# Issuing the last store of a batched matmul-subtract from ScalarE's queue, behind the main section

## The chip, the cores and the metric

The kernel runs on one core of a Trainium2 chip. The metric is the device time of one execution in microseconds (us). Runs of the kernel are given by their median; one further execution was recorded by the hardware profiler, and all times inside the kernel come from that recording.

## The reference

```python
def setup_inputs():
    batch, m, k, n = 16, 512, 1024, 768
    return {
        "x": np.random.randn(batch, m, k).astype(np.float32),
        "weight": np.random.randn(k, n).astype(np.float32),
        "sub_value": np.random.randn(batch, m, n).astype(np.float32),
    }

def reference(x, weight, sub_value):
    return (np.matmul(x, weight) - sub_value).astype(np.float32)
```

One weight matrix is shared by the whole batch, so this is a product of 8192 x 1024 by 1024 x 768 with an elementwise subtraction behind it.

## The kernel before

The 8192 rows are cut into 64 tiles of 128 rows. For each tile, `x` comes in as float32; ScalarE casts it to float16 (line 324); TensorE transposes it (line 342) and ScalarE copies the result back (line 355), or, for some pairs of tiles, VectorE transposes it in blocks (line 375). TensorE then multiplies it with the resident float16 weights into a PSUM accumulator (lines 199 and 404). VectorE subtracts (line 424): it reads the accumulator and the tile's `sub_value` from `so_ring` and writes the result over `sub_value` in the same ring. The result is stored from there.

All transfers are listed in `TRANSFERS`, in the order in which they are issued: kind (`x`, `w` for the weights, `s` for `sub_value`, `o` for the output), first tile, number of tiles. `issue()` goes down this list and puts each transfer on SyncE's queue (line 304; line 264 for the weights). A store waits for the count of subtractions, `finish`. The last three stores are five tiles (56 to 60, 1920 KB), two tiles (61 and 62, 768 KB) and one tile (63, 384 KB). In a store, each row of a tile goes to its own place in the output, 128 partitions at a time.

Besides these, ScalarE issues one small transfer at the very start (line 177): 16 rows of 128 bytes from `sub_value` into the output, which later stores overwrite. The stores wait for it (`touched`).

Each transfer raises a semaphore by 16 when it has landed: each of the 16 DMA engines raises it by one. `lane` hands out these semaphores and takes one again when the transfers that used it are known to have landed; `known` collects those. At the end of the kernel, the lanes that hold transfers not yet known to have landed are `left`; one of them, `last`, is that of the last store.

The instructions are first collected per engine and then written out in one critical section (`section`), whose waits are all placed by hand. When a section closes, SyncE signals the other engines; each of them passes a drain (GpSimd a no-op) and signals back; SyncE waits for all of these and passes on. Behind the sections the framework adds a closing part: SyncE drains, all engines meet in a barrier, GpSimd clears the semaphores, and all meet once more.

Before the change, SyncE waits inside the main section for all of `left` but `last` (line 531), then closes the section (line 532), and waits for `last` alone in a second section that only SyncE has work in (lines 533 and 534). In the profile, the waits of the second section and the closing part carry line 560, and some of the signals of the sections the lines 137 and 533.

Of the kernel before, what the change touches and what calls it, by code (L numbers as in the profile page):

```python
# [104 lines left out]
def kernel(  # L105
# [7 lines left out]
    nc = tc.nc  # L113
# [7 lines left out]
    n_mt = M_TOT // P  # L121
# [5 lines left out]
    def view(flat, at, n):  # L127

        first, size = next(one for one in SEGMENTS if one[0] <= at < sum(one))
        assert at + n <= first + size  # L130
        rows = flat[first * P : (first + size) * P].rearrange("(p j) c -> p j c", p=P, j=size)
        return rows[:, at - first : at - first + n]
# [36 lines left out]
    def count(name):  # L169
        so_far[name] += 1  # L170
        return (counter[name], 1)
# [11 lines left out]
        out=along, data0=ones, data1=ones, initial=0.0, op0=mybir.AluOpType.mult, op1=mybir.AluOpType.add,  # L183
    ), waits=[(counter["ident"], 1)], then=count("ident"))
    dve.add(lambda: nc.vector.transpose(across, along), waits=[(counter["ident"], 3)], then=count("ident"))  # L185
    for a in range(P // Q):
        here = slice(a * Q, (a + 1) * Q)
        dve.add(lambda here=here: nc.vector.tensor_tensor(  # L188
            out=ident[here, here], in0=along[here], in1=across[here], op=mybir.AluOpType.is_equal,
# [33 lines left out]
    todo = list(TRANSFERS)  # L223
# [3 lines left out]
    lanes = []  # L227
    of_x, of_s, of_o = {}, {}, {}
    known = set()

    def lane(tag):

        for one in lanes:
            if one["tags"] <= known:
                break
        else:
            one = {"sem": tc.alloc_semaphore(f"lane{len(lanes)}"), "value": 0, "tags": set()}
            lanes.append(one)
        one["value"] += 16
        one["tags"].add(tag)  # L240
        return one["sem"], one["value"]

    def issue():
        nonlocal known, from_w
        while todo:
            kind, at, n = todo[0]
            span = set(range(at, at + n))
            old = {t - NX if kind == "x" else t - NSO for t in span}
            need, by = {
                "w": (set(), "o"),  # L250
                "x": ({t for t in old if t >= 0}, "cast"),
                "s": ({t for t in old if t >= 0}, "o"),
                "o": (span, "finish"),
            }[kind]
            if not need <= done[by]:
                return
            todo.pop(0)
            done[kind] |= span
            if kind == "w":

                first = NSO - 2 * (n_c - at)
                st = so_ring[:, first : first + 2 * n]
                sem, value = lane((kind, at))
                sp.add(lambda st=st, at=at, n=n: nc.sync.dma_start(out=st, in_=w_rows[:, 2 * at : 2 * (at + n)]), then=(sem, 16))  # L264
                for c in range(at, at + n):
                    for r in range(2):
                        here = so_ring[:, first + 2 * (c - at) + r]
                        dve.add(
                            lambda c=c, r=r, here=here: nc.vector.tensor_copy(out=w_sb[:, c, r], in_=here),  # L269
                            waits=[(sem, value)], then=count("w"),  # L270
                        )
                        staged[first + 2 * (c - at) + r] = so_far["w"]
                    w_at[c] = so_far["w"]
                from_w |= {(("w", at), so_far["w"])}
                continue
            ring, size, flat = {
                "x": (x_ring, NX, x_flat), "s": (so_ring, NSO, sub_flat), "o": (so_ring, NSO, out_flat)
            }[kind]
            here = ring[:, at % size : at % size + n]
            there = view(flat, at, n)  # L280
            waits = []
            if kind == "x" and need:
                waits.append((counter["cast"], max(cast_at[t] for t in need)))
                last = max(need, key=lambda t: cast_at[t])
                known |= {tag for t, tag in of_x.items() if t in cast_at and cast_at[t] <= cast_at[last]}
            if kind == "s":
                for t in need:
                    waits.append(landed["o", t])
                    known.add(of_o[t])
                for t in span:  # L290
                    if t % NSO in staged:
                        waits.append((counter["w"], staged.pop(t % NSO)))
                        known |= {tag for tag, value in from_w if value <= waits[-1][1]}
            if kind == "o":
                waits.append((touched, 16))
                waits.append((counter["finish"], max(finish_at[t] for t in need)))
                known |= {of_s[t] for t in finish_at if finish_at[t] <= max(finish_at[u] for u in need)}
            sem, value = lane((kind, at))
            for t in span:
                landed[kind, t] = (sem, value)  # L300
                {"x": of_x, "s": of_s, "o": of_o}[kind][t] = (kind, at)
            if kind == "o":
                here, there = there, here
            sp.add(lambda here=here, there=there: nc.sync.dma_start(out=here, in_=there), waits, (sem, 16))  # L304

    def cast(mi):
        assert mi in done["x"]
        done["cast"].add(mi)
        x_in = x_ring[:, mi % NX].rearrange("p (q c r) -> p c q r", c=n_c, r=2)
        first = mi - mi % 2  # L310
        waits = [landed["x", mi]]
        if first in ON_DVE:
            if mi == first:
                b, before = take("x16p", N16P, mi)
                if before is not None:
                    waits.append((counter["pair"], pair_at[before]))
            to = x16p_b[:, slot["x16p", first], mi - first]
        else:
            b, before = take("x16", N16, mi)
            if before is not None:  # L320
                waits.append((counter["turn"], turn_at[before]))
            to = x16_b[:, b]
        to = to.rearrange("p (c q r) -> p c q r", c=n_c, r=2)
        act.add(lambda: nc.scalar.copy(out=to, in_=x_in), waits, count("cast"))  # L324
        cast_at[mi] = so_far["cast"]
        issue()
# [92 lines left out]
    def finish(mi):  # L419
        assert mi in done["s"]  # L420
        done["finish"].add(mi)
        o = so_ring[:, mi % NSO].rearrange("p (h n) -> p h n", h=2)
        po = po_b[:, slot["po", mi]]
        dve.add(lambda: nc.vector.tensor_tensor(  # L424
            out=o, in0=po[:, :, :NS], in1=o, op=mybir.AluOpType.subtract
        ), [landed["s", mi], (counter["mul"], mul_at[mi])], count("finish"))
        finish_at[mi] = so_far["finish"]
        issue()

    issue()  # L430


# [91 lines left out]
    pe.emit_loop([pe.ops[a:b] for a, b in zip(ends, ends[1:])])  # L524
    pe.emit(pe.ops[ends[-1] :])

    left = [one for one in lanes if not one["tags"] <= known]
    last = next(one for one in left if of_o[n_mt - 1] in one["tags"])
    for one in left:
        if one is not last:  # L530
            nc.sync.wait_ge(one["sem"], one["value"])
    section.close()
    with tc.tile_critical(sync_engine=mybir.EngineType.SP, no_gpsimd_drain=True):
        nc.sync.wait_ge(last["sem"], last["value"])


# [28 lines left out]
```

## Time and profile before

| what | value |
| --- | --- |
| median of 5 runs | 210.3 us (209.95 to 210.35) |
| profiled execution | 210.22 us |
| its span, first to last instruction | 208.4 us |
| TensorE matmul busy | 196.3 us (94%) |
| VectorE busy | 128.0 us (61%) |
| ScalarE busy | 113.6 us (55%) |
| bytes moved, mean rate | 87.08 MB, 418 GB/s |

The span is what the recording shows of the program's own instructions; the execution's time holds 1.82 us more, which lie around it. Times inside the profile count from the start of the span. Lines such as `L304` are lines of the kernel; `SPq` is SyncE's sequencer (it issues transfers and waits), `ACTq` ScalarE's. A DMA row gives the time from issue to landing, that is, until the semaphore has its full count.

### The profile page before, as it was taken

How to read it: one execution, taken by the hardware profiler on the slowest of the kernel's cores; microseconds unless marked ns; L12 is line 12 of the kernel's file. 1: busy time of each engine (PE TensorE's matmuls, PEld its weight loads, DVE VectorE, ACT ScalarE, POOL GpSimd, SP SyncE). 2: the span in 40 equal slices, each digit the busy share in tenths (PEclk: the TensorE clock that was granted, in tenths of full speed). 3: DMA queues.
4: the chain of work that ended last, by engine and by line, in shares of the span. 5: the costliest groups of instructions: out<-in, count | busy, mean ns of one | idle time of the engine just before them, and what ended most of it. 6: DMA issues, size and time to landing. Idle time of an engine off the chain costs nothing.

```text
span 208.4 us, 2609 instructions
## 1 busy us (share of the span) xinstructions
PE 196.3 (94%) x1233; PEld 75.6 (36%) x701; DVE 128.0 (61%) x224; ACT 113.6 (55%) x113; POOL 1.0 (0%) x7
## 2 busy tenths in 40 slices
PE   6989699989999999999999999999999999999970
PEld 0133334324434433443443443343344344334320
DVE  2321513975994795598299479559829937953330
ACT  4274688616772862845655586293665738607300
POOL 1000000000000000000000000000000000000000
PEclk9999999999999999999999999999999999999996
DMA  6999999999999899999999999999999999999993
GB/s 214 392 448 417 440 428 424 429 421 451 453 410 478 370 453 434 450 421 407 467 434 418 425 420 439 437 453 415 417 459 418 437 429 415 443 434 425 432 409 145
DMA packets 4932, 87.08 MB, mean 418 GB/s; under 512 B 576, under 2 KB 576, under 8 KB 960
## 3 DMA queue, kind: packets, MB, share of 16 engines
q1 hardware_dynamic: 4896, 87.03, 97.8%
q8 instruction: 1, 0.02, 0.0%
q14 instruction: 3, 0.02, 0.0%
q10 hardware_dynamic: 32, 0.00, 0.0%
HBM read 61.87 MB, written 25.17 MB: 418 GB/s over the span
## 4 chain that ended last, share of the span: by engine, by line
PE 75%; DMA 14%; DVE 6%; SPq 2%; issue 1%; DVEq 0%
PE po_b L199 67%; DMA so_ring<-in_sub_value_dram 14%; PE pt_b L342 8%; DVE xtp_b L375 3%; DVE so_ring L424 2%; SPq L304 1%; SPq L264 0%; SPq L560 0%; DVEq L58 0%; SPq L137 0%
## 5 line engine op out<-in xcount | busy, mean ns | idle before, releaser
L199 PE MATMUL po_b<-w_sb,xt_b 128*128 128x384 f16 x704 | 125.8, 326 | 1.8 <-DVE so_ring L424 1.4
L424 DVE TENSOR_TENSOR so_ring<-po_b,so_ring 128x768 f32<-128x768 f32 x64 | 60.8, 957 | 60.9 <-PE po_b L199 41.9
L355 ACT COPY xt_b<-pt_b 128x1024 f16<-128x1024 f16 x44 | 44.4, 1012 | 62.6 <-PE pt_b L342 62.6
L375 DVE STREAM_TRANSPOSE xtp_b<-x16p_b 32x256 f32<-32x256 f32 x144 | 62.7, 435 | 2.5 <-ACT x16p_b L324 0.3
L199 PE MATMUL po_b<-w_sb,xtp_b 128*128 128x384 f16 x320 | 61.3, 326 | 1.1 <-DVE xtp_b L375 1.0
L404 PEld LDWEIGHTS <-xt_b 128*128 128x128 f16 x352 | 34.4, 98 | 59.0 <-issue 54.0
L324 ACT CAST x_b<-x_ring 128x1024 f16<-128x1024 f32 x46 | 50.6, 1126 | 7.6 <-DMA x_ring<-in_x_dram 7.6
L342 PE MATMUL pt_b<-ident,x_b 128*128 128x128 f32 x184 | 47.4, 274 | 1.1 <-ACT x_b L324 1.1
L342 PEld LDWEIGHTS pt_b<-ident,x_b 128*128 128x128 f32 x184 | 25.3, 141 | 44.9 <-issue 39.4
L324 ACT CAST x16p_b<-x_ring 128x1024 f16<-128x1024 f32 x18 | 20.3, 1126 | 11.0 <-DMA x_ring<-in_x_dram 11.0
L404 PEld LDWEIGHTS <-xtp_b 128*128 128x128 f16 x160 | 15.7, 98 | 19.7 <-issue 17.6
L199 PE MATMUL po_b<-idle_x,idle_w 128*128 128x512 f16 x25 | 8.8, 504 | 1.7 <-POOL idle_x L179 1.7
L269 DVE CAST w_sb<-so_ring 128x768 f16<-128x768 f32 x8 | 3.9, 554 | 10.2 <-DMA so_ring<-in_weight_dram 10.2
L355 ACT COPY xtp_b<-pt_b 128x1024 f16<-128x1024 f16 x2 | 2.0, 1014 | 1.4 <-PE pt_b L342 1.4
L324 ACT ACT_TABLE_LOAD x1 | 1.3, 1283 | 1.6 <-SPq L137 1.6
L434 PEld LDWEIGHTS <-idle_w 128*128 128x128 f16 x5 | 0.5, 99 | 2.1 <-POOL idle_x L179 1.7
L188 DVE TENSOR_TENSOR ident<-along,across 32x32 f32<-32x32 f32 x4 | 0.7, 183 | 0.1
L180 DVE MEMSET ones<- 128x32 f32 x1 | 0.1, 85 | 1.0 <-SPq L137 1.0
L179 POOL MEMSET idle_x<- 128x512 f16 x1 | 0.5, 529 | 0.0
L506 ACT CAST stub<-ident 128x1 f16<-128x1 f32 x2 | 0.4, 192 | 0.0
L185 DVE STREAM_TRANSPOSE across<-along 128x32 f32<-128x32 f32 x1 | 0.2, 211 | 0.0
L483 POOL MEMSET mark<- 128x1 f32 x1 | 0.1, 98 | 25.1 <-ACT xtp_b L355 25.1
(7 smaller groups left out, 1.0 us busy)
## 6 DMA issues: line engine op xcount, KB each, us to landing
so_ring<-in_sub_value_dram SPq DMA_DIRECT2D x7, 3072.0 KB, 24.2
out_dram<-so_ring SPq DMA_DIRECT2D x7, 3072.0 KB, 26.0
x_ring<-in_x_dram SPq DMA_DIRECT2D x5, 4096.0 KB, 22.6
x_ring<-in_x_dram SPq DMA_DIRECT2D x2, 2048.0 KB, 29.4
so_ring<-in_weight_dram SPq DMA_DIRECT2D x2, 1536.0 KB, 9.8
x_ring<-in_x_dram SPq DMA_DIRECT2D x3, 1024.0 KB, 20.6
so_ring<-in_sub_value_dram SPq DMA_DIRECT2D x2, 1536.0 KB, 24.1
x_ring<-in_x_dram SPq DMA_DIRECT2D x1, 3072.0 KB, 27.4
```

Source lines behind the costliest of these rows:

```text
L179: pool.add(lambda: nc.gpsimd.memset(idle_x, 0.0), then=count("idle"))
L188: dve.add(lambda here=here: nc.vector.tensor_tensor(out=ident[here, here], in0=along[here], in1=across[here], op=mybir.AluOpType.is_equal, ...
L199: return nc.tensor.add_instruction(mybir.InstMatmult(name=nc.get_next_instruction_name(), engine=full.engine, ins=list(full.ins), outs=lis ...
L269: lambda c=c, r=r, here=here: nc.vector.tensor_copy(out=w_sb[:, c, r], in_=here),
L304: sp.add(lambda here=here, there=there: nc.sync.dma_start(out=here, in_=there), waits, (sem, 16))
L324: act.add(lambda: nc.scalar.copy(out=to, in_=x_in), waits, count("cast"))
L342: pe.add(lambda: nc.tensor.transpose(words, from_, ident), waits, count("turn") if last else None)
L355: act.add(lambda: nc.scalar.copy(out=to, in_=pt_b[:, b]), waits, count("evac"))
L375: dve.add(lambda: nc.vector.transpose(xt[b * Q : (b + 1) * Q, :, a * Q : (a + 1) * Q], x16[a * Q : (a + 1) * Q, :, b * Q : (b + 1) * Q],), ...
L404: pe.add(lambda weights=weights: nc.tensor.ldweights(weights, tile_position=(0, 0)), [w for w in waits if w[0] in ready])
L424: dve.add(lambda: nc.vector.tensor_tensor(out=o, in0=po[:, :, :NS], in1=o, op=mybir.AluOpType.subtract), [landed["s", mi], (counter["mul"] ...
L434: pe.add(lambda: nc.tensor.ldweights(idle_w, tile_position=(0, 0)), [(counter["idle"], 2)])
```

## The change

The last entry of `TRANSFERS` is no longer put on SyncE's queue. `issue()` keeps its source and destination in `outside` and takes no lane for it. The main section closes without waiting for any store. A second section, named `waited`, follows, in which SyncE waits for every lane that is not known to have landed. After it the kernel issues the last store from ScalarE with a plain `dma_start` that the framework tracks: the framework gives it a semaphore of its own, and SyncE's drain in the closing part waits for that semaphore. `add_manual_dep` puts the store behind `waited` in the order of the program without a wait on it (`NoSync`).

```diff
@@ -227,6 +227,7 @@
     lanes = []
     of_x, of_s, of_o = {}, {}, {}
     known = set()
+    outside = []
 
     def lane(tag):
 
@@ -295,6 +296,9 @@
                 waits.append((touched, 16))
                 waits.append((counter["finish"], max(finish_at[t] for t in need)))
                 known |= {of_s[t] for t in finish_at if finish_at[t] <= max(finish_at[u] for u in need)}
+            if kind == "o" and not todo:
+                outside[:] = there, here
+                return
             sem, value = lane((kind, at))
             for t in span:
                 landed[kind, t] = (sem, value)
@@ -524,14 +528,17 @@
     pe.emit_loop([pe.ops[a:b] for a, b in zip(ends, ends[1:])])
     pe.emit(pe.ops[ends[-1] :])
 
-    left = [one for one in lanes if not one["tags"] <= known]
-    last = next(one for one in left if of_o[n_mt - 1] in one["tags"])
-    for one in left:
-        if one is not last:
-            nc.sync.wait_ge(one["sem"], one["value"])
     section.close()
-    with tc.tile_critical(sync_engine=mybir.EngineType.SP, no_gpsimd_drain=True):
-        nc.sync.wait_ge(last["sem"], last["value"])
+    with tc.tile_critical(sync_engine=mybir.EngineType.SP, no_gpsimd_drain=True) as waited:
+        for one in lanes:
+            if not one["tags"] <= known:
+                nc.sync.wait_ge(one["sem"], one["value"])
+    here, there = outside
+    stored = nc.scalar.dma_start(out=here, in_=there)
+    tc.add_manual_dep(
+        stored.ins, waited.name, mybir.DependencyInfo(mybir.DependencyClass.NoSync, mybir.DependencyReason.DATA),
+        reason="behind the waits",
+    )
 
 
 # ---- launch: one core; inputs and outputs as the reference has them ----
```

In the built program ScalarE's store waits for the count with which SyncE ends the main section, and for nothing else. Behind the second section's waits, SyncE has one branch, one signal, one drain, one no-op and the drain that waits for the last store.

## The prediction

> **What bounds the kernel now.** I read the page first, then the timeline of the last 15 us, the DMA issues, the busy time in short stretches, and SyncE's own waits.
>
> ```profile
> span 208.4 us, 2609 instructions
> PE 196.3 (94%) x1233; PEld 75.6 (36%) x701; DVE 128.0 (61%) x224; ACT 113.6 (55%) x113; POOL 1.0 (0%) x7
> GB/s 214 392 448 417 440 428 424 429 421 451 453 410 478 370 453 434 450 421 407 467 434 418 425 420 439 437 453 415 417 459 418 437 429 415 443 434 425 432 409 145
> q10 hardware_dynamic: 32, 0.00, 0.0%
> PE 75%; DMA 14%; DVE 6%; SPq 2%; issue 1%; DVEq 0%
> ```
>
> TensorE is 94% busy and the DMA engines move some 430 GB/s until the last slices. The change touches nothing before the last subtraction, so only the end matters: what lies behind it.
>
> The timeline (start, duration, engine and line):
>
> ```profile
> 201.91 0.96 DVE L424 TENSOR_TENSOR so_ring<-po_b,so_ring 128x768 f32<-128x768 f32 x1 [1.64 <-PE po_b L199]
> 202.90 0.33 SPq L304 DMA_DIRECT2D out_dram<-so_ring  x1
> ```
>
> The last subtraction ends at 202.87; SyncE starts the last store at 202.90. From there to the end, 208.40, no compute engine is busy. The DMA issues (KB each, us from issue to landing):
>
> ```profile
> out_dram<-so_ring SPq DMA_DIRECT2D x1, 1920.0 KB, 9.8
> out_dram<-so_ring SPq DMA_DIRECT2D x1, 768.0 KB, 5.9
> out_dram<-so_ring SPq DMA_DIRECT2D x1, 384.0 KB, 4.2
> out_dram<-in_sub_value_dram ACTq DMA_DIRECT2D x1, 2.0 KB, 3.6
> ```
>
> The five-tile store (issued 194.55) lands at 204.3, the two-tile store (200.30) at 206.17, the one-tile store (202.90) at 207.12. Busy time by stretch, the last two columns being the DMA share and GB/s:
>
> ```profile
> 204.00:205.00 1.00, 0.00 (x0) 0.00 (x0) 0.00 (x0) 0.00 (x0) 0.00 (x0) 0.95 0.80 323
> 205.00:206.00 1.00, 0.00 (x0) 0.00 (x0) 0.00 (x0) 0.00 (x0) 0.00 (x0) 0.50 0.19 77
> 206.00:207.00 1.00, 0.00 (x0) 0.00 (x0) 0.00 (x0) 0.00 (x0) 0.00 (x0) 0.50 0.08 34
> ```
>
> A share of 0.19 is three of the 16 DMA engines, 0.08 little more than one. In the packet records, 13 engines' shares of the last store land between 205.03 and 205.51, the other three at 206.57, 206.94 and 207.12; the two earlier stores split the same way (three engines 1.1 to 1.7 us behind the rest). So the end hangs on one late DMA engine working off its queue: its share of the five-tile store until 203.98, eight 6,144-byte packets of the two-tile store until 205.82 (0.234 us each), eight 3,072-byte packets of the last until 206.78 (0.121 each), and 0.34 to the landing. SyncE's waits:
>
> ```profile
> SPq L531 <- DMA out_dram<-so_ring: 2.8, 1, 2.8
> SPq L304 <- DVE so_ring L424: 2.3, 1, 2.3
> SPq L560 <- DMA out_dram<-so_ring: 0.2, 1, 0.2
> ```
>
> SyncE sleeps 2.8 us for the two-tile store (L531), closes the main section (206.25 to 206.92), then sleeps 0.16 for the last store. After the landing at 207.12 it still passes a branch (207.18), a signal (207.33), a drain (207.42), a no-op (207.49), a drain (207.54) and the barrier drain (207.60). From there the barrier and the clearing of semaphores take 0.80, to 208.40: landing to end 1.28.
>
> **The change, part by part.** In the built program everything up to the two-tile store is the same, instruction for instruction.
>
> 1. *The last store leaves SyncE's queue and is issued by ScalarE after a handshake.* SyncE closes the section as soon as the two-tile store is issued (200.63) and waits for the drains of the other engines; VectorE's is last, behind the subtraction (202.87). No row shows a VectorE drain behind work; GpSimd's at the start ended 0.05 after its last memset, so 202.92. A semaphore reaches another engine in about 0.03 (the subtraction's end to the store's start: 0.028), so SyncE goes on at 202.95. Two event waits and a no-op, 0.065 apart in the same place of this trace (206.578, 206.642, 206.708), put its signal at 203.09, and ScalarE starts at 203.12: 0.22 later than now. ScalarE has been idle since its last copy (197.8). Nothing is queued behind its wait but the store and the final barrier.
>
> 2. *The issue itself on ScalarE's queue.* The one ScalarE issue of this trace:
>
> ```profile
> L177 ACTq DMA_DIRECT2D out_dram<-in_sub_value_dram x1: 619/619/619, 0.9 to 0.9; - x1
> ```
>
> It took 0.62, where SyncE's first took 0.38 and its late ones 0.33. Bounds: no longer than SyncE's (0.33), or 0.29 more. First packets now come 0.85 after the issue started (203.745), so they come at 203.96 to 204.25. I take 204.1, since the 0.62 was that engine's first. On the 13 quick engines the last store then lands 0.2 to 0.5 later, by 206.0 at most. This costs nothing on the path: the late engine reaches the last store only at 205.83, at least 1.6 after the packets are there. If that cover is gone (all engines level), the 0.22 to 0.51 is paid.
>
> 3. *Two queues instead of one on each DMA engine.* Same bytes, same engines, so the late engine still runs dry near 206.78 and the last of the two stores still lands at 207.12; only the order between them can change. ScalarE's 32 packets at the start (ring 10 on the page) are the row for this. They were issued at 0.90, the first started at 3.593, and on each engine they began as the eight packets of the first load of x ended (3.587 to 4.00), never between them. I therefore take it that a started store is finished first. At 204.1 the late engine has left the five-tile store (203.98) and is inside the two-tile store, so the order stays: two-tile lands 206.17, last 207.12. The margin is 0.12, and -0.02 to 0.27 at the bounds.
>
> The Trainium skill ("DMA: Bandwidth & Descriptors", Queues, rings and completion order) states that each DMA engine goes round its queues and drains a whole packet of some 9 to 17 descriptors before it switches. That speaks against the change: whatever ScalarE queues while an engine is still in the five-tile store would, by the rule, be served before the two-tile store. With arrival at 204.1 the rule gives the same sum as the row, with arrival before 203.98 the sum of the first rival below.
>
> 4. *SyncE's second section waits for the other stores.* Wake-up at 206.185 (two-tile store), five more event waits 0.064 apart (+0.32), branch +0.064, signal +0.155, drain +0.085, no-op +0.073, final drain +0.044: 206.93. It lies under the last store's flight, with 0.19 to spare.
>
> 5. *The end waits only in the final drain.* Landing 207.12, +0.015 to wake, +0.063 to the barrier drain, +0.80: 208.00. Before: 208.40.
>
> The sum: -0.40 (1.28 from landing to end becomes 0.88), with 0.22 to 0.51 of later issue hidden. Span 208.00; the profiled execution took 210.22 for a span of 208.40, so 1.82 lies around it: **209.82**. The median of the runs is 210.30, 0.08 above the profiled one; the same saving from the median would be 209.90.
>
> **The rivals.**
>
> *The last store overtakes the two-tile store on the late engine.* Place: ring order on that one engine. It decides if the packets arrive before the engine leaves the five-tile store (203.98 here, against 203.96 to 204.25), or if engines mix two stores packet by packet. Price: the last store's eight packets go first (0.97), so the two-tile store lands at up to 207.12, and behind it now stands the whole of step 4 (0.76) and the barrier (0.86): end 208.74, +0.34, **210.56**. Mixed packet by packet from 204.1, seven small packets come between: landing near 207.02, end 208.64, 210.46. For it: the margin is smaller than the 0.4 by which runs differ. Against: the start of the kernel shows no mixing, and every cost that I left out of step 1 makes the arrival later.
>
> *ScalarE's queue is slow.* Its one transfer needed 2.69 from issue to first packet; I read that as waiting for x. If it is the queue's own, packets start at 205.81 and the last lands at 207.13 to 207.54 (spread of 0.41 as at the start): 208.0 to 208.4, **209.82 to 210.24**.
>
> *The late engine is not late* in the timed runs. Then 205.51 is the landing before, the 0.22 to 0.51 is paid, and the sum is -0.18 to +0.11: **210.04 to 210.33**. Against: the same three engines' lag shows in all three stores.
>
> *The store really waits for the second section.* ScalarE would issue at about 206.8, landing 2.2 later (0.85, eight packets, 0.34) and 0.88 to the end: 209.9, **211.7**. Against: in the built program ScalarE's store waits for the count that SyncE raises at the end of the first section.
>
> **How the numbers follow.** Chances: forecast 0.60, overtaking 0.20, slow queue 0.11, level engines 0.07, waiting store 0.02. A measurement of this kernel tells 0.2% (0.42 us) from no change, so the bounds are 209.88 and 210.72. The forecast lies right at the first: 209.82 to 209.90, so I give it 0.39 faster and 0.21 same. Overtaking, at 210.56 on the profiled execution and 210.64 on the median, is half same, half slower (0.10 each). Slow queue: 0.03 faster, 0.06 same, 0.02 slower. Level engines same. Waiting store slower. Faster 0.42, same 0.44, slower 0.14. Range: the forecast less 0.3 for the runs' own spread (209.95 to 210.35 before), up to the overtaking case: 209.5 to 210.6; the forecast's own is 209.6 to 210.0.
>
> **What would show it.** ScalarE's store at 203.1 with a duration of 0.33 to 0.62; the two-tile store landing near 206.2 and before the last one; the last still at 207.1; then under 0.9 to the end, and SyncE's last DMA wait in the closing part rather than at L531. If the two-tile store lands within 0.7 of the last or after it, step 3 is wrong; if the last lands after 207.3, step 2 is; if more than 0.95 lies between landing and end, step 5 is.

## The result, and the profile after

| what | before | after |
| --- | --- | --- |
| median | 210.2 us (209.88 to 210.8, 49 runs) | 209.79 us (209.4 to 210.24, 29 runs) |
| ratio, after to before | | 0.9981, 95% interval 0.9976 to 0.9987 |
| profiled execution | 210.22 us, span 208.4 us | 210.04 us, span 208.2 us |

The kernel is 0.19% faster, 0.40 us of 210.2 (0.27 to 0.50 by the interval). The two profiled executions differ by only 0.18 us. That is no contradiction: in the recording of after, the late DMA engine ran 0.22 us later than in that of before, as shown below, and one recording is one draw.

The timeline of after (start, duration, engine and line), where lines 308 and 428 are the old lines 304 and 424:

```profile
200.75 0.33 SPq L308 DMA_DIRECT2D out_dram<-so_ring  x1
202.36 0.96 DVE L428 TENSOR_TENSOR so_ring<-po_b,so_ring 128x768 f32<-128x768 f32 x1 [1.64 <-PE po_b L199]
203.57 0.36 ACTq L537 DMA_DIRECT2D out_dram<-so_ring  x1
```

The last subtraction ends at 203.32 (202.87 in the recording of before), and ScalarE starts the last store 0.25 behind it, where SyncE started it 0.03 behind. The DMA issues of the three last stores (KB, us from issue to landing):

```profile
out_dram<-so_ring SPq DMA_DIRECT2D x1, 1920.0 KB, 9.5
out_dram<-so_ring SPq DMA_DIRECT2D x1, 768.0 KB, 5.6
out_dram<-so_ring ACTq DMA_DIRECT2D x1, 384.0 KB, 3.8
```

200.75 + 5.6 puts the two-tile store's landing at 206.39, 203.57 + 3.8 the last one's at 207.34: the order has stayed, 0.95 apart as before, and both are 0.22 later than before (206.17 and 207.12). Busy time by stretch, the last two columns being the DMA share and GB/s:

```profile
205.00:206.00 1.00, 0.00 (x0) 0.00 (x0) 0.00 (x0) 0.00 (x0) 0.00 (x0) 0.95 0.50 203
206.00:207.00 1.00, 0.00 (x0) 0.00 (x0) 0.00 (x0) 0.00 (x0) 0.00 (x0) 0.50 0.12 49
```

The 13 quick DMA engines now work on the last store until 205.5 (share 0.50 instead of 0.19 in the first row), because its packets came later. Behind 206 only late engines are left, as before (a share of 0.12 is two of the 16 on average; before it was 0.08). The quick engines lost time that nobody waits for. SyncE's waits:

```profile
SPq L535 <- DMA out_dram<-so_ring: 2.8, 1, 2.8
SPq L137 <- DVEq L137: 2.1, 1, 2.1
SPq L567 <- DMA out_dram<-so_ring: 0.2, 1, 0.2
```

L137 is the close of the main section: SyncE waits there for VectorE's drain, before the store and not behind it. L535 is the two-tile store in the second section, and the last row the final drain, which now waits for the last store itself. Its row, with the barrier drain behind it:

```profile
L567 SPq DRAIN  x3: 7/7/7, 207.4 to 207.7; - x3
```

The first of the three is that drain, at 207.354 in the record, and the end is at 208.213. From landing to end: 208.213 - 207.337 = 0.88, where before had 208.396 - 207.118 = 1.28. The difference, 0.40, is the saving that the timed runs show.

### The profile page after: what moved, and what is told of

It is laid out like the page before. It is cut to its first block, busy times and chain, and to the rows that moved or that the text cites. A ratio compares the mean times of both kernels' runs of the same rounds, so it can differ in the third digit from the quotient of the medians.

```text
span 208.2 us, 2608 instructions
## 1 busy us (share of the span) xinstructions
PE 196.3 (94%) x1233; PEld 76.1 (37%) x701; DVE 128.0 (61%) x224; ACT 113.5 (55%) x113; POOL 1.0 (0%) x7
## 4 chain that ended last, share of the span: by engine, by line
PE 89%; DMA 5%; ACT 2%; DVE 0%; SPq 0%; issue 0%
PE po_b L199 80%; PE pt_b L346 9%; DMA x_ring<-in_x_dram 5%; ACT x_b L328 2%; ACT xt_b L359 0%; DVE so_ring L428 0%; ACT xtp_b L359 0%; SPq L265 0%; SPq L308 0%; SPq L567 0%; SPq L137 0%
## 5 line engine op out<-in xcount | busy, mean ns | idle before, releaser
L199 PE MATMUL po_b<-w_sb,xt_b 128*128 128x384 f16 x704 | 127.3, 329 | 3.2 <-DVE w_sb L270 1.8
L199 PE MATMUL po_b<-idle_x,idle_w 128*128 128x512 f16 x25 | 7.6, 445 | 1.7 <-POOL idle_x L179 1.7
```

Source lines behind the costliest of these rows:

```text
L199: return nc.tensor.add_instruction(mybir.InstMatmult(name=nc.get_next_instruction_name(), engine=full.engine, ins=list(full.ins), outs=lis ...
```

## The experiments

Ratios are to the kernel before, timed on the same chip in the same rounds. The spread of a single ratio is about 0.001 either way, 0.2 us.

**ScalarE's queue alone.** In `issue()` of the kernel before, the last store goes to ScalarE, inside the main section:

```diff
+            if kind == "o" and not todo:
+                act.add(lambda here=here, there=there: nc.scalar.dma_start(out=here, in_=there), waits, (sem, 16))
+                return
             sp.add(lambda here=here, there=there: nc.sync.dma_start(out=here, in_=there), waits, (sem, 16))
```

> The kernel before, with one thing changed: the last store is issued by ScalarE inside the main section, as soon as the last subtraction is counted; waits and closing as before. Theory (the change saves 0.40 us because five steps of SyncE between the last landing and the end are gone; ScalarE's queue itself saves nothing): landing to end stays 1.28 us. If the two queues are served in order of arrival, ratio 1.000 to the kernel before (+0.0 us). If an engine takes turns between the queues, the last store's packets come at about 203.75, before the latest DMA engine leaves the five-tile store (203.98), the last store overtakes the two-tile store there, the two-tile store lands near 207.1, and 2.1 us of closing follow it: end near 209.2, +0.8 us, ratio 1.004. Rival (ScalarE's queue, a second queue beside SyncE's, is what saves): -0.4 us, ratio 0.998.

Ratio 1.0000 (0.9991 to 1.0009). The issue and its landing:

```profile
202.62 0.36 ACTq L305 DMA_DIRECT2D out_dram<-so_ring  x1
out_dram<-so_ring ACTq DMA_DIRECT2D x1, 384.0 KB, 4.9
```

Landing 207.51, end 208.79: 1.28 again. ScalarE's queue saves nothing. The DMA view of this kernel, between the issue and 203.8:

```profile
q1 hardware_dynamic: 76, 0.45, 89.2%
q10 hardware_dynamic: 14, 0.04, 8.8%
```

ScalarE's packets (ring 10) are on the quick engines by then, from 203.59. The latest engine leaves the five-tile store only at 204.38 in this recording. So the packets did come first, and still the two-tile store landed at 206.58 and the last at 207.51. Nothing overtook anything: of the expectation's two branches the one with order of arrival holds here.

**The moved waits alone.** All stores stay on SyncE; the second section waits for all of them:

```diff
-    left = [one for one in lanes if not one["tags"] <= known]
...
     section.close()
     with tc.tile_critical(sync_engine=mybir.EngineType.SP, no_gpsimd_drain=True):
-        nc.sync.wait_ge(last["sem"], last["value"])
+        for one in lanes:
+            if not one["tags"] <= known:
+                nc.sync.wait_ge(one["sem"], one["value"])
```

> The kernel before, with the waits for all stores, the last one's too, moved into the second section; all stores stay on SyncE's queue inside the main section. Theory: the handshake of the main section now runs early, but behind the last landing (207.12) stand the wake, five more event waits (0.32), branch, signal, drain, no-op, drain (0.42) and the closing (0.86): landing to end 1.62, +0.34 us, ratio 1.0016. Rival (the early handshake of the main section is what saves): -0.4 us, ratio 0.998.

Ratio 1.0016 (1.0007 to 1.0025), +0.34 us. This half of the change is a loss by itself. SyncE's rows for the second section and the closing:

```profile
L531 SPq EVENT_SEMAPHORE  x2: 17/22/28, 206.7 to 207.7; - x2
...
L557 SPq EVENT_SEMAPHORE  x7: 17/28/28, 207.7 to 209.2; - x7
L557 SPq DRAIN  x3: 7/7/7, 208.4 to 208.7; - x3
```

The wait for the last store ends at 207.67. Five of the event waits of L557 come behind it, 0.06 apart, where nothing hides them (the other two belong to the closing). Landing (207.653) to end (209.265) is 1.61.

**A tracked store on SyncE.** The changed kernel, with the store issued between the sections:

```diff
     section.close()
-    with tc.tile_critical(sync_engine=mybir.EngineType.SP, no_gpsimd_drain=True) as waited:
+    here, there = outside
+    nc.sync.dma_start(out=here, in_=there)
+    with tc.tile_critical(sync_engine=mybir.EngineType.SP, no_gpsimd_drain=True):
...
```

> The changed kernel with the last store issued as a tracked transfer by SyncE, between the main section and the second one. The framework then puts a wait for it at the end of the second section's waits. Theory: issue about 0.2 us later than in the kernel before, hidden by the late DMA engine (landing 207.1); behind the landing stand branch, signal, drain, no-op and two drains again, 1.28 us to the end: +0.0 us, ratio 1.000. Rival (a tracked transfer is what saves, wherever it is waited for): -0.4 us, ratio 0.998. Rival (the later issue costs): +0.2 us, ratio 1.001.

Ratio 0.9995 (0.9986 to 1.0004): no difference to the kernel before. The store was issued 0.28 behind the subtraction and landed at 207.32, the two-tile store 0.95 ahead of it; landing to end 1.32. So tracking is not what saves. It saves only if nothing but the last drain waits for it. Here the framework also put a wait for it into the second section, at its end (at 207.337 in the record), with branch, signal, drain and no-op behind it. SyncE's two waits there, for the two-tile store and for the last one:

```profile
SPq L537 <- DMA out_dram<-so_ring: 2.8, 1, 2.8
SPq L563 <- DMA out_dram<-so_ring: 0.6, 1, 0.6
```

On SyncE the store could stand behind that section only by being issued after its waits, that is, after 206.4. This is what ScalarE's queue is for in the change.

**One more microsecond in front of the store.** The changed kernel, with copies on ScalarE behind the last subtraction, into buffers that nobody reads any more (`n` is 1, then 3):

```diff
     assert not todo
     marks[n_mt] = len(pe.ops)
+    for b in range(n):
+        act.add(lambda b=b: nc.scalar.copy(out=x16_b[:, b], in_=x_ring[:, 0]), [(counter["finish"], so_far["finish"])])
```

> The changed kernel with one more copy of 128x1024 (1.0 to 1.1 us) on ScalarE between the last subtraction and the end of the main section, so that the last store is issued about 1.1 us later. Theory (a late DMA engine reaches the last store only about 1.7 us after its packets are there, so a delay up to that costs nothing): same as the changed kernel, -0.4 us to the kernel before, ratio 0.998, last landing as early as without the copy. Rival (the delay is on the path): +0.7 us to the kernel before, ratio 1.003.

Ratio 0.9979 (0.9970 to 0.9988): as fast as the changed kernel. SyncE waits 0.99 longer for ScalarE's drain, the store is issued 1.21 behind the subtraction, and still lands at 207.10, end 207.98. The delay is hidden.

> The changed kernel with three more copies of 128x1024 (3.0 to 3.4 us in all) on ScalarE between the last subtraction and the end of the main section. Theory: the cover of about 1.7 us is used up; packets come at about 207.1 to 207.4, landing 1.3 us later near 208.5, end near 209.4, +1.0 us to the kernel before (ratio 1.005): of the delay of 3.1 about 1.4 is paid. Rival (the delay is paid whole): +2.7 us, ratio 1.013.

Ratio 1.0018 (1.0006 to 1.0029), +0.38 us. A part of the delay is paid, but less than expected (+1.0). Its profile shows that the cover is used up:

```profile
203.42 2.94 ACT L521 CAST x_b<-x_ring 128x1024 f16<-128x1024 f32 x3 [5.13 <-DVE so_ring L428]
206.49 0.36 ACTq L539 DMA_DIRECT2D out_dram<-so_ring  x1
```

and, by stretch:

```profile
206.00:207.00 1.00, 0.00 (x0) 0.00 (x0) 0.00 (x0) 0.36 (x1) 0.00 (x0) 0.55 0.00 0
207.00:208.00 1.00, 0.00 (x0) 0.00 (x0) 0.00 (x0) 0.00 (x0) 0.00 (x0) 0.50 0.66 267
```

All 16 engines stand still for a microsecond (share 0.00) and then do the last store together, landing 2.3 after its issue. The timed runs pay 0.38 + 0.40 = 0.78 of 2.89 against the changed kernel, so they have a cover of 2.1 (1.8 to 2.4 by the two intervals), not the 1.6 that the recording of after gives (packets at 204.43, the latest engine done with the two-tile store at 206.05; the expectation took 1.7). The recording of this run, with the subtraction as late as 203.39, is the slowest of its nine runs (211.49 us, median 210.97).

**Another cut of the last stores.** To see whether the last store overtakes, the tail was cut into six, one and one tiles, so that the latest engine stays longer in the first of them; in the changed kernel and in the kernel before:

```diff
-    ('o', 24, 8), ('o', 32, 8), ('s', 56, 8), ('o', 40, 8), ('o', 48, 8), ('o', 56, 5),
-    ('o', 61, 2), ('o', 63, 1),
+    ('o', 24, 8), ('o', 32, 8), ('s', 56, 8), ('o', 40, 8), ('o', 48, 8), ('o', 56, 6),
+    ('o', 62, 1), ('o', 63, 1),
```

> The changed kernel with the stores at the end cut as six tiles, one tile, one tile instead of five, two, one; same bytes. The latest DMA engine leaves the six-tile store at about 204.9, after the last store's packets are there (204.1). Theory with turns between the queues: on that engine the last store goes ahead of tile 62's store, which then lands last, near 207.1, and 1.62 us follow it: end near 208.7, +0.3 us to the kernel before, ratio 1.0016. Theory with service in order of arrival: tile 62's store lands near 206.2 and the last at 207.1, end 208.0, -0.4 us, ratio 0.998.

> The kernel before with the stores at the end cut as six tiles, one tile, one tile; all on SyncE's queue. The control for the run before it: tile 62's store lands about 0.95 us ahead of the last one, landing to end 1.28; same time as the kernel before within 0.1 us (ratio 1.000), because the late engine has the same bytes in the same order.

Ratios 0.9977 (0.9967 to 0.9987) and 1.0002 (0.9992 to 1.0012). In the first, ScalarE issued at 202.70, the latest engine left the six-tile store at 205.08, tile 62's store landed at 206.37 and the last at 207.31. The three last stores:

```profile
out_dram<-so_ring SPq DMA_DIRECT2D x1, 2304.0 KB, 8.3
out_dram<-so_ring SPq DMA_DIRECT2D x1, 384.0 KB, 6.5
out_dram<-so_ring ACTq DMA_DIRECT2D x1, 384.0 KB, 4.6
```

Again the order stays, although the last store's packets were due at 203.57 (0.87 after the issue, as on an idle engine), 1.5 us before that.

**Small transfers in the middle of the kernel.** The kernel before, with four transfers of 2 KB from ScalarE into a buffer that nobody reads, behind the casts of tiles 24, 32, 40 and 48:

```diff
...
+            if t in (24, 32, 40, 48) and t - lead(t) == mi:
+                act.add(lambda t=t: nc.scalar.dma_start(out=probe[:, t // 8 - 3], in_=sub_flat[:: M_TOT // 16, :Q]), then=(probed, 16))
...
+    nc.sync.wait_ge(probed, 64)
```

> The kernel before with four transfers of 2 KB issued by ScalarE in the middle of the kernel into a buffer nobody reads, while SyncE's queue holds several transfers (20 to 30 us from issue to landing). Theory with turns between the queues: each lands after at most one of SyncE's transfers has been finished on each engine, 2 to 9 us from issue to landing. Theory with service in order of arrival: 20 us or more. It also shows ScalarE's issue time when it is not the first: 0.33 to 0.40 us, against 0.62 at the start. The time is not compared.

The DMA issues of this kernel:

```profile
so_ring<-in_sub_value_dram SPq DMA_DIRECT2D x7, 3072.0 KB, 24.2
out_dram<-so_ring SPq DMA_DIRECT2D x7, 3072.0 KB, 26.4
...
probe<-in_sub_value_dram ACTq DMA_DIRECT2D x4, 2.0 KB, 6.1
```

Here ScalarE's transfers do pass SyncE's: 6.1 us against 24 to 26. Their first packets start 3.5 to 3.7 after the issue, on the last engine up to 5.1, in most places between two packets of one and the same transfer. ScalarE's issue takes 0.317 to 0.363, so with this shape the 0.62 belongs to the kernel's first issue. Another shape can take as long later: the 104-row part in the last experiment took 0.61.

**A deep queue at the end.** The two findings together suggest that an engine has some packets lined up that later ones cannot pass, and takes turns behind these. The changed kernel with `('o', 56, 7)` and then `('o', 48, 8)` in front of the last store, both issued at 200.3 to 201.1:

> The changed kernel with the stores at the end in another order, so that much more stands on SyncE's queue when ScalarE's last store comes: seven tiles (56 to 62) and then eight tiles (48 to 55), both issued after the subtraction of tile 62, about 14 us of packets on each DMA engine. Theory (an engine has some 2.6 to 4.2 us of packets lined up, ScalarE's come in behind these and then by turns with SyncE's): the first packets of the last store start 3.5 to 5 us after its issue, near 207 to 208, and the store lands before SyncE's last one. Theory (arrival order at the end of the kernel): first packets only when SyncE's stores are through, near 215, and the last store lands last. The time itself is longer, some 8 us, because the stores start late; it is not compared.

```profile
q1 hardware_dynamic: 80, 1.97, 89.4%
q10 hardware_dynamic: 80, 0.25, 11.9%
```

This is the DMA view between 208.2 and 213.3: 80 packets from each queue, one for one. Between 203.0 and 207.5 (the store is issued at 203.12) it shows SyncE's alone:

```profile
q1 hardware_dynamic: 80, 1.72, 89.0%
```

The last store's first packets start at 207.55, 4.4 after the issue, on each engine between the last data packet of the seven-tile store and that store's closing four-byte packet; it lands at 215.37 and SyncE's eight-tile store, issued 2.4 us earlier, at 216.27. So overtaking exists, packet by packet, but only after a wait of some 3.6 us (4.4 less the 0.87 of an idle engine).

**A search for a faster version.** The last store cut into partitions 0 to 103 and 104 to 127, in the hope that the late engines are left out:

```diff
...
-    stored = nc.scalar.dma_start(out=here, in_=there)
+    for part in (slice(0, 104), slice(104, 128)):
+        stored = nc.scalar.dma_start(out=here[part], in_=there[part])
...
```

> The changed kernel with the last store cut into two tracked transfers on ScalarE's queue: partitions 0 to 103, then 104 to 127. A search for a faster version: a transfer of 104 rows may use 13 DMA engines with 8 rows each and one of 24 rows 12 engines with 2 each, so that some engines get nothing of the last store. If the three late engines are among those left out, the last landing moves from about 207.2 to about 206.2 and the end waits for the two-tile store instead (landing 206.2 to 206.4, then 0.76 and 0.86): -0.15 to -0.25 us to the changed kernel, -0.6 us to the kernel before, ratio 0.997. If the late engines are among those used, they get 10 rows instead of 8: +0.24 us to the changed kernel, -0.15 us to the kernel before, ratio 0.999. If the rows are spread otherwise, no difference to the changed kernel but for a second issue of 0.36 us that the late engines hide: ratio 0.998.

Ratio 0.9989 (0.9979 to 0.9999), 0.17 us slower than the changed kernel by the two ratios, which lies inside their intervals (+0.24 was expected for this case). In the second transfer's landings three stragglers stand out (206.75, 207.31, 207.65), with the rest by 206.50: the late engines are among those used, and got more rows. A part of the loss is SyncE's: with two tracked transfers the framework puts one more wait (for the second part, at 207.67) in front of the final drain, and landing to end is 0.95 instead of 0.88. No version was found that is measurably faster than the changed kernel.

## Why the prediction was right

The prediction was 209.82 us and the median is 209.79; the sum, -0.40, is what the ratio gives. That the two times agree to 0.03 is partly luck: by the median that the prediction had (210.30, five runs) the same saving gives 209.90, and the recording of after took 210.04.

One of the prediction's own signs of being wrong did appear: the last store landed at 207.34, and "after 207.3" was to mean that step 2 is wrong. It wasn't step 2. The two-tile store, which the change doesn't touch, landed 0.22 later too, so the late engine was later in this recording. In the other recordings where the last store isn't delayed on purpose, and is one transfer, it lands at 207.12 to 207.65, so the sign was set too tight.

1. *The handshake before the store* (0.22 later): measured 0.246 - 0.028 = 0.22. The assumed 0.05 for VectorE's drain behind work was about right: SyncE went on 0.08 after the subtraction, as assumed. (The store itself came at 203.57, not 203.1, because the subtraction ended 0.45 later in this recording.)
2. *The issue on ScalarE* (0.33 to 0.62): 0.357, and the first packets 0.87 after it started. That is 1.11 behind the subtraction, 0.02 over the lower bound; the value taken, 0.14 over it, was too careful.
3. *The order of the two stores.* The outcome was right, by luck, and the reason was wrong. The step said that a started store is finished first and that the margin is 0.12. Turns are taken packet by packet (the deep queue, the small transfers), yet in the run with ScalarE's queue alone and in the six-one-one cut the packets came before the latest engine left the store in front, and nothing was overtaken. What probably protects the order here is that only 2.5 to 2.7 us of packets stood ahead on that engine, while ScalarE's packets waited 2.6 to 4.2 us where more stood ahead (3.5 to 5.1 from issue to first packet, less the 0.87 that an idle engine needs). That there is such a line, and that its length is what decides, is inferred from these waits and not shown by a row of its own; the two ranges touch, and no run has a tail just long enough to be overtaken. The rule of turns of the Trainium skill ("DMA: Bandwidth & Descriptors", Queues, rings and completion order) says that an engine goes round its queues, and the runs agree. It has the engine drain a packet of some 9 to 17 descriptors before it switches. In the profile each of these stores is nine packets on an engine, one for each of eight partitions and a closing one of four bytes, and the deep queue alternates after each single one (80 and 80). If such a packet is one descriptor, which no row says, the runs switch sooner than the page has it. Where SyncE's queue was deep they also show no switch for the first 2.6 us and more.
4. *SyncE's second section under the store's flight* (0.19 to spare): woken at 206.41, its last no-op at 207.10, the last store at 207.34. As predicted.
5. *Landing to end* 0.88: measured 0.88. The moved waits show the price of the same steps when they stand behind the landing (1.61), and the tracked store on SyncE (1.32) that the tracking alone doesn't bring it.

The cover was sized at 1.6 or more from one recording. It is 2.1 in the timed runs. In the recordings where the store isn't delayed on purpose, the late engine reaches the last store 1.6 to 2.7 us after its packets are there, because the subtraction's end moves (202.45 to 203.32) and the late engine's landing of the store in front moves less, and not with it (206.17 to 206.71). The subtraction ends latest in the two recordings whose granted clock falls to half for 3.4 us near 25 us (203.32 after, 203.39 with three copies); in the others it ends at 202.45 to 202.95, with no such fall before it, and no row shows why it varies there.

The level-engines rival falls with the same numbers: timed runs that have a cover of 2.1 have a late engine. The slow-queue rival falls with the first packets, 0.87 after the issue, and the waiting-store rival with the issue at 203.57, nearly 3 us before the second section's first wait ends. The prediction read the split of the two earlier stores as 1.1 to 1.7 us; the landings give 1.06 to 1.60, and nothing rests on it.

## What to carry to other kernels

At the end of a kernel, count the steps between the landing of the last transfer and the last instruction, and let that landing be awaited by the very last of them; here five steps of SyncE were worth 0.40 us, and a later issue was free because one late DMA engine still had 2 us to do. Moving half of such a change can cost: the moved waits alone were 0.34 us slower, and the second queue alone brought nothing. A transfer from a second queue can pass what stands on the first (it did in the deep queue), but not at once: here it waited 2.6 to 4.2 us for its turn, and where only 2.5 to 2.7 us stood ahead it passed nothing.

## What the hardware showed

- The last store's 16 shares do not land together: three DMA engines trail, the last of them 1.2 to 2.1 us behind the thirteenth in the landings of the store in front of it. Where the engines first stood still (three copies; the deep queue), all 16 land within 0.2 us, even after 14 us of packets in the deep queue. So the lag of the last engine is a backlog carried along, not a slower rate. In the recording of before, the last engine is 0.11 us behind the thirteenth in the transfer that lands at 29.28, 1.51 in the next one, which lands at 34.37, and 1.3 to 1.7 from there to the end.
- The subtraction's end moved by 0.9 us between recordings of kernels with the store on time (202.45 with the six-one-one cut, 203.32 after), and the last landing did not follow it (207.31 and 207.34).
- Between the landings at 29.28 and 34.37, at 31.15, one engine works 0.93 us on a packet of 16 KB that is none of the kernel's transfers. The DMA view of before from 31.0 to 32.1 has it as

```profile
q8 instruction: 1, 0.02, 5.3%
```

In all twelve recordings there is one such packet (at 31.15 to 35.06), and in all twelve it falls between the two landings at which the lag appears. A second engine's lag comes the same way (0.10 us at 48.90, 0.89 at 56.15 in the recording of before, with an `instruction` packet of 8 KB on queue 14 at 50.74). So the late engine that hides the later issue is probably a trace of such packets; no experiment removed them, and the third engine's lag, which grows from 0.01 at 163.33 to 1.06 at 204.31, has no row that explains it.
